# Start-up of a two-layer encoder: input transfers in tile pairs, squares and their sum off POOL, bias table with its rows outermost

## The chip, the core and the metric

The kernel runs on one core of a Trainium2 chip. The metric is the device time of one execution in microseconds (us). A core has five engines with an instruction queue each: PE (TensorE, matrix multiplies, whose weight loads are shown as PEld), DVE (VectorE), ACT (ScalarE), POOL (GpSimd) and SP (SyncE, which issues all DMA transfers here). Sixteen DMA engines carry the transfers.

## The reference

An encoder of two layers over 512 positions of width 1024, all in float32. What matters for this change is the first layer's mixer:

```python
h = x
for l in range(DEPTH):
    hn = rms_norm(h, norm_mix[l])
    if l % 2 == 0:
        ...
        h = h + even_mixer(hn, w_in_even[e], w_out_even[e], lam, ...)
    else:
        h = h + odd_mixer(hn, w_in_odd[o], sg_norm[o], sg_w[o], sg_b[o], w_out_odd[o])
    h = h + swiglu(rms_norm(h, norm_ffn[l]), w_ffn_in[l], w_ffn_out[l])
return rms_norm(h, norm_final)
```

`even_mixer` projects the normed input to eight streams. Four heads go through a gated recurrence in two directions (queries, two gates `zf` and `zb`, values), four through differential attention with a bias by relative position: `bias = rel_bias[rel_bucket(k_pos - q_pos)]`. `rms_norm` needs the mean of the squares over all 1024 features of each position.

## The kernel before, in words

Features lie on the partitions: a tile is 128 features by 512 positions, and the input `xT` is eight such tiles, stored as four pairs. Every product is made of three matmuls of 128x128 by 128x512, since each float32 operand is split into a high part (`fp32r`, cast on ACT) and a low part (a subtraction on DVE): high by high, high by low, low by high. The weights are split on the chip in the same way as they arrive: `weight` (L360) issues a transfer of 512 KB into `raw`, casts it to `whi` and subtracts to `wlo`; for the first weight this is done in two halves, each with a transfer of its own (L367 to L375).

Nothing is issued in the order of the source. `Plan.op` (L80) records each operation with an engine, an estimated cost, the tiles that it reads and writes, and a priority; `Plan.schedule` (L110) then runs a model of the five queues and writes out the order of each engine, the lowest priority number first among what is ready, with limited numbers of tiles of each kind. A DMA counts as its size over 360 KB/us and is taken to land 2 us later. Operations with `port` set are kept apart in the model between DVE and POOL (L189). Without a priority an operation has its place in the source; transfers of weight `i` have -1e6 + 10 i. The first part of the kernel is made of:

- L350: the table `colt` (gains, 25 KB) is loaded ahead of the plan.
- L528 to L533: the input, eight transfers of 256 KB, with priorities among those of the first three weights. Each tile goes to `Norm.add` (L488), which makes the split of x times its gain (`x_m`: ACT, L502, then DVE, L503) and calls `Norm.square` (L507).
- `Norm.square`: for the first two tiles of the first norm the square is a multiply on POOL (L510), else an ACT instruction (L512). The sum over eight tiles is six adds on POOL (L518) and a last one on DVE (L520). The same class serves all four norms ahead of the mixers and feed-forward layers (`m0`, `f0`, `m1`, `f1`). For the first norm the squares and adds have priority 150, so they come after everything of that stage.
- `rstat` (L417): the sum goes over the partitions on PE (`st_m`), then a power on POOL and a product that spreads the result (`sp_m`), which becomes `R_m`, the scale by which all projections are multiplied.
- L535 to L575: masks, lambdas and the one-hot table are loaded, and the bias of each head by relative position is made by two small products `u` into `ut` (4 rows of 1024).
- `store_table` (L577): `ut` goes to DRAM as `ud` (4 x 1024), and one transfer DRAM to DRAM writes it 128 times as `um` (4 heads x 128 rows x 1024, 2 MB). Both sides of that transfer have the 4 heads outermost. The attention heads read skewed rows of `um` far later.
- `gla` (L587) is called for two heads (projections q, zf, zb of 8 steps with 3 matmuls each); then `values` (L720) projects the values `vi` from the four parts of `wev`, 512 KB each; `gla_core` (L598) is a long chain of small steps (`km` on ACT, `lv` on PE, `W` on DVE and POOL, `att` on DVE).

All transfers stand in SP's one queue in the planned order.

Of the kernel before, what the change touches and what calls it, by code (L numbers as in the profile page):

```python
# [13 lines left out]
ALU = mybir.AluOpType  # L14
# [200 lines left out]
def encoder_kernel(  # L215
# [131 lines left out]
    um = dp.tile([4, P, D], F32, name="um")  # L347
    hgn = colt[:, 41:42]

    nc.sync.dma_start(colt, cols)  # L350
    make_identity(nc, ident)
    G.memset(ones, 1.0)
    G.memset(mhalf, -0.5)
# [6 lines left out]
    def weight(src):  # L360
        i = weights[0]
        weights[0] += 1
        n = src.shape[-1]
        raw = buf("raw", f"raw{i}")
        hi = buf("whi", f"whi{i}", F32R)
        lo = buf("wlo", f"wlo{i}", F32R)
        step = n // 2 if i == 0 else n  # L367
        for c in range(0, n, step):
            pr = -1e6 + i * 10 + c * 0.005
            cut = lambda ap, c=c: ap[:, c:c + step]  # L370
            pa = c // step if step < n else None
            dma(raw(cut, pa), src[:, c:c + step], step / 2, prio=pr, after=gate)
            acopy(hi(cut, pa), raw(cut, pa), cost=0.16 + step * 0.00078, prio=pr)
            vtt(lo(cut, pa), raw(cut, pa), hi(lambda ap, c=c: f32(ap)[:, c:c + step], pa), ALU.subtract,
                cost=0.07 + step * 0.00104, prio=pr, either=True)  # L375
        hi.half = lo.half = step < n
        return hi, lo
# [104 lines left out]
    class Norm:  # L482
# [5 lines left out]
        def add(self, h, prio=None):  # L488
            k = self.n
            if self.paired:  # L490
                if k % 2 == 0:
                    self.b = buf("huge", f"b_{self.name}{k}", shape=(P, 8, H))
                s0 = 2 - 2 * (k % 2)
                act(self.b(lambda ap: ap[:, s0:s0 + 2].rearrange("p a c -> p (a c)"), part=1 - k % 2), h, AF.Copy, scale=colt[:, self.gain * KC + k:self.gain * KC + k + 1],
                    cost=0.61, prio=URGENT + len(plan.ops))
                if k % 2:
                    self.xs.append(operands(self.b, f"{self.name}{k}"))
                self.square(h, prio)
                return
            g = colt[:, self.gain * KC + k:self.gain * KC + k + 1]  # L500
            xp = buf("big", f"x_{self.name}{k}", F32R)
            act(row(xp, 0), h, AF.Copy, scale=g, cost=0.61)  # L502
            vstt(row(xp, 1), h, g, frow(xp, 0), ALU.mult, ALU.subtract)  # L503
            self.xs.append(xp)
            self.square(h, prio)

        def square(self, h, prio=None):  # L507
            sq = buf("tmp", f"sq_{self.name}{self.n}")
            if self.gain == 0 and self.n < 2:
                gtt(sq, h, h, ALU.mult, prio=prio)  # L510
            else:
                act(sq, h, AF.Square, prio=prio)  # L512
            self.n += 1
            if self.sq is None:
                self.sq = sq
                return
            if self.n < KC:
                gtt(self.sq, self.sq, sq, ALU.add, prio=prio)  # L518
                return
            vtt(self.sq, self.sq, sq, ALU.add)  # L520
            if self.gain in (0, 2):
# [3 lines left out]
            else:  # L525
                self.R = rnorm(self.sq, D, self.name, "R")

    n0 = Norm(0, "m0")  # L528
    for j in range(KC // 2):
        xt = buf("big", f"xin{j}")  # L530
        for i in range(2):
            dma(row(xt, i), xT[j][:, i], 256, prio=-1e6 + (0.5, 2, 3, 11, 12, 21, 22, 23)[2 * j + i])
            n0.add(row(xt, i), 150)  # L533

    maskf = buf("big", "maskf", shape=(P, 7, P))  # L535
    dma(maskf, masks, 448, prio=-1e6 + 95)
# [22 lines left out]
    lt = buf("tmp", "lt", shape=(P, 256))  # L559
    lprod = buf("tmp", "lprod", shape=(P, 128))  # L560
    dma(lt, lams.partition_broadcast(P), 128, prio=-1e6 + 96)
    op_tiny = plan.op("DVE", 2.0, tiny, [lprod], [lt])

    oht, ut = buf("big", "oht", shape=(P, D)), buf("big", "ut", shape=(P, D))

# [10 lines left out]

    def store_table():  # L577
        nc.sync.dma_start(ud, ut.ap()[0:4])
        nc.sync.dma_start(um, bass.AP(ud.tensor, ud.offset, [[D, 4], [0, P], [1, D]]))

    op_um = plan.op("DMA", 6.0, store_table, [], [ut], prio=200)

# [639 lines left out]
```

## Time and profile before

| | |
|---|---|
| median of 3 runs | 1203.88 us (1202.47 to 1203.91) |
| the profiled execution, its own time | 1204.61 us |
| its span in the trace | 1202.8 us |
| PE busy | 1163.3 us, 97% |
| DVE busy | 915.4 us, 76% |
| ACT busy | 579.1 us, 48% |
| POOL busy | 188.0 us, 16% |
| moved by DMA | 118.58 MB, mean 99 GB/s |
| granted TensorE clock, mean | 0.995 |

The span runs from the first instruction to the last; the time of the execution is 1.8 us longer. An engine is busy while an instruction of it runs; idle time is put down to what ended it. In the views below a line such as "7.04 1.65 PE L329 MATMUL q<-x_m,whi ... x2 [7.04 <-ACT x_m L322]" reads: at 7.04 us, for 1.65 us, on PE, two instructions from line 329 that write `q` and read `x_m` and `whi`; in brackets how long the engine had been idle and what it waited for.

### The profile page before, as it was taken

To read this page: it belongs to the slowest core of one execution; us is meant where nothing else is said; L and a number is where in the kernel's file an instruction comes from. 1 tells how busy PE (TensorE), PEld (TensorE's weight loads), DVE (VectorE), ACT (ScalarE), POOL (GpSimd) and SP (SyncE) were. 2 spreads that over 40 slices of the span, in tenths; PEclk is the share of its full clock that TensorE was granted. 3 is DMA by queue.
4 is the path that set the end of the run, shared out by engine and by line. 5 is a ranking of instruction groups with operands and counts; after the bars stand their busy time and mean duration, and the time that the engine had idled before them with its cause. 6 is when DMAs were issued, how large, how long until landed. Compare 5 with 4: busy or idle time off the path is not lost.

```text
span 1202.8 us, 17650 instructions
## 1 busy us (share of the span) xinstructions
PE 1163.3 (97%) x7072; PEld 1031.0 (86%) x7072; DVE 915.4 (76%) x1304; ACT 579.1 (48%) x881; POOL 188.0 (16%) x185
## 2 busy tenths in 40 slices
PE   6989999999999999999999999999999999999997
PEld 3868888778778999999999888878899999999996
DVE  5467698769697997777777873757799778877874
ACT  5244465657554544444444444335555444444444
POOL 4355584213130000000000040003000000000003
PEclk9989999999999999999999999999999999999998
DMA  6420420343415232424233423330333232323302
GB/s 217 165 82 1 111 81 10 91 123 88 158 35 174 81 106 70 141 71 141 71 140 106 141 78 98 88 105 5 148 110 133 71 132 79 108 102 106 105 1 71
DMA packets 28686, 118.58 MB, mean 99 GB/s; under 512 B 5272, under 2 KB 7448, under 8 KB 20412
## 3 DMA queue, kind: packets, MB, share of 16 engines
q1 hardware_dynamic: 28604, 117.46, 29.5%
q8 instruction: 55, 0.90, 0.3%
q14 instruction: 27, 0.22, 0.1%
HBM read 115.30 MB, written 4.23 MB: 99 GB/s over the span
## 4 chain that ended last, share of the span: by engine, by line
PE 80%; DMA 7%; DVE 6%; issue 4%; ACT 2%; POOL 1%; SPq 0%; POOLq 0%; DVEq 0%; ACTq 0%
PE fo_0b L329 8%; PE fo_0a L329 8%; PE uo L329 4%; PE oo L329 4%; PE vo L329 3%; PE lv L657 2%; DMA raw<-wev 2%; PE fo_18a L329 2%; PE vi L329 2%; PE last L329 1%; PE q L329 1%; PE zf L329 1%; PE zb L329 1%; PE oe L329 1%; DMA xin<-xT 1%
## 5 line engine op out<-in xcount | busy, mean ns | idle before, releaser
L298 DVE TENSOR_TENSOR wlo<-raw,whi 128x1024 fp32r<-128x1024 f32 (+1 forms) x65 | 85.4, 1314 | 29.5 <-ACT whi L317 29.4
L298 DVE TENSOR_TENSOR lb<-comb,hb 128x1024 fp32r<-128x1024 f32 x44 | 53.7, 1220 | 38.5 <-ACT hb L317 38.5
L317 ACT CAST whi<-raw 128x1024 fp32r<-128x1024 f32 (+1 forms) x65 | 66.8, 1031 | 22.3 <-DMA raw<-wev 10.7
L298 DVE TENSOR_TENSOR la<-raw,ha 128x1024 fp32r<-128x1024 f32 x44 | 55.0, 1249 | 27.1 <-ACT ha L317 26.9
L317 ACT CAST hb<-comb 128x1024 fp32r<-128x1024 f32 x44 | 46.1, 1048 | 59.7 <-PE pa9a L948 2.4
L310 POOL TENSOR_TENSOR sq_m<-sq_m,sq_m 128x512 f32<-128x512 f32 x12 | 19.9, 1657 | 328.9 <-ACT sq_m L322 328.4
L317 ACT CAST ha<-raw 128x1024 fp32r<-128x1024 f32 x44 | 46.2, 1049 | 48.8 <-PE pa10a L948 2.4
L298 DVE TENSOR_TENSOR l<-raw,h 128x1024 fp32r<-128x1024 f32 (+1 forms) x48 | 54.5, 1136 | 17.0 <-ACT h L317 15.4
L317 ACT CAST hc<-comb 128x1024 fp32r<-128x1024 f32 x44 | 46.1, 1047 | 37.3 <-PE fo_0b L329 15.5
L298 DVE TENSOR_TENSOR comb<-comb,raw 128x512 f32<-128x512 f32 x88 | 62.4, 709 | 0.1
L317 ACT CAST h<-raw 128x1024 fp32r<-128x1024 f32 (+1 forms) x48 | 46.6, 975 | 27.9 <-PE pb4b L948 2.0
L310 POOL TENSOR_TENSOR sq_fin<-sq_fin,sq_fin 128x256 f32<-128x256 f32 x12 | 8.9, 738 | 327.2 <-ACT sq_fin L322 326.8
L687 POOL TENSOR_TENSOR W<-W,T 128x512 f32<-128x512 f32 x38 | 52.7, 1394 | 39.7 <-PE lv L657 35.5
L298 DVE TENSOR_TENSOR lc<-comb,hc 128x1024 fp32r<-128x1024 f32 x44 | 54.7, 1244 | 2.2 <-ACT hc L317 2.2
L924 DVE TENSOR_TENSOR comb<-raw 128x1024 f32<-128x1024 f32 x44 | 54.7, 1243 | 0.0
L329 PE MATMUL vo<-whi,x_m 128*128 128x512 f32 x128 | 40.3, 391 | 0.1
L329 PE MATMUL uo<-x_m,whi 128*128 128x512 f32 x128 | 40.1, 394 | 0.0
L329 PE MATMUL oo<-mx,whi 128*128 128x512 f32 x128 | 39.6, 390 | 0.0
L657 PEld LDWEIGHTS lv<-W,km 128*128 128x128 f32 x224 | 31.4, 196 | 8.6 <-ACT km L650 6.2
L317 ACT CAST hd<-raw 128x512 fp32r<-128x512 f32 x44 | 27.4, 622 | 22.4 <-PE pa0a L948 2.0
L657 PE MATMUL lv<-W,km 128*128 128x128 f32 x224 | 32.5, 290 | 5.8 <-ACT km L650 5.8
L310 POOL TENSOR_TENSOR sq_f<-sq_f,sq_f 128x512 f32<-128x512 f32 x12 | 20.2, 1686 | 103.1 <-ACT sq_f L322 103.1
(2624 smaller groups left out, 4208.7 us busy)
## 6 DMA issues: line engine op xcount, KB each, us to landing
raw<-wfi SPq DMA_DIRECT2D x44, 1024.0 KB, 4.9
raw<-wfo SPq DMA_DIRECT2D x20, 1024.0 KB, 4.9
raw<-we SPq DMA_DIRECT2D x23, 512.0 KB, 5.2
raw<-wev SPq DMA_DIRECT2D x8, 512.0 KB, 12.4
raw<-woe SPq DMA_DIRECT2D x8, 512.0 KB, 3.8
raw<-wov SPq DMA_DIRECT2D x8, 512.0 KB, 3.7
raw<-wo SPq DMA_DIRECT2D x8, 512.0 KB, 3.6
raw<-woo SPq DMA_DIRECT2D x8, 512.0 KB, 3.7
```

The costliest lines, as they stand in the source:

```text
L298: return plan.op("DVE", cost, lambda: V.tensor_tensor(use(o), use(a), use(b), op), [o], [a, b], prio=prio, after=after, alt=alt, port=insi ...
L310: return plan.op("POOL", cost, lambda: G.tensor_tensor(use(o), use(a), use(b), op), [o], [a, b], prio=prio)
L317: return plan.op("ACT", cost, lambda: A.copy(use(o), use(a)), [o], [a], prio=prio)
L329: T.matmul(use(o), lhsT=use(l), rhs=use(r), start=s0, stop=s1)
L657: T.matmul(blk(ps.ap(), b), lhsT=blk(km.ap(), b), rhs=mixed(0, b * P, P, s)(W.ap()), start=True, stop=True)
L687: return lambda: eng.tensor_tensor(view(W.ap()), view(W.ap()), fn(TT.ap()), ALU.mult)
L924: plan.op("DVE", 1.14, lambda: V.tensor_tensor(comb.ap()[:, 0:2], raw.ap()[:, 0:1].broadcast_to([P, 2, S]), raw.ap()[:, 1:3], ALU.add), [c ...
```

## The change

Four things are edited. The first weight is loaded by one transfer and still split in two halves. `colt` becomes a planned transfer right behind it (`op_cols`), on which the first uses of `colt` depend. The input comes in four transfers of a tile pair, 512 KB each, with priorities 0.5, 6, 11 and 12 (the second and third weight have 10 and 20), and the squares and adds of the first norm get priority 20 in place of 150. All squares are made on ACT and all adds on DVE, in all four norms of this class. The DRAM to DRAM transfer to `um` has the 128 rows outermost on both sides, and the 4 heads inside them; the rows themselves (4 KB each, 512 of them) stay.

```diff
@@ -347,7 +347,6 @@
     um = dp.tile([4, P, D], F32, name="um")
     hgn = colt[:, 41:42]
 
-    nc.sync.dma_start(colt, cols)
     make_identity(nc, ident)
     G.memset(ones, 1.0)
     G.memset(mhalf, -0.5)
@@ -369,7 +368,8 @@
             pr = -1e6 + i * 10 + c * 0.005
             cut = lambda ap, c=c: ap[:, c:c + step]
             pa = c // step if step < n else None
-            dma(raw(cut, pa), src[:, c:c + step], step / 2, prio=pr, after=gate)
+            if c == 0:
+                dma(raw, src, n / 2, prio=pr, after=gate)
             acopy(hi(cut, pa), raw(cut, pa), cost=0.16 + step * 0.00078, prio=pr)
             vtt(lo(cut, pa), raw(cut, pa), hi(lambda ap, c=c: f32(ap)[:, c:c + step], pa), ALU.subtract,
                 cost=0.07 + step * 0.00104, prio=pr, either=True)
@@ -499,23 +499,20 @@
                 return
             g = colt[:, self.gain * KC + k:self.gain * KC + k + 1]
             xp = buf("big", f"x_{self.name}{k}", F32R)
-            act(row(xp, 0), h, AF.Copy, scale=g, cost=0.61)
+            act(row(xp, 0), h, AF.Copy, scale=g, cost=0.61).deps.add(op_cols)
             vstt(row(xp, 1), h, g, frow(xp, 0), ALU.mult, ALU.subtract)
             self.xs.append(xp)
             self.square(h, prio)
 
         def square(self, h, prio=None):
             sq = buf("tmp", f"sq_{self.name}{self.n}")
-            if self.gain == 0 and self.n < 2:
-                gtt(sq, h, h, ALU.mult, prio=prio)
-            else:
-                act(sq, h, AF.Square, prio=prio)
+            act(sq, h, AF.Square, prio=prio)
             self.n += 1
             if self.sq is None:
                 self.sq = sq
                 return
             if self.n < KC:
-                gtt(self.sq, self.sq, sq, ALU.add, prio=prio)
+                vtt(self.sq, self.sq, sq, ALU.add, prio=prio)
                 return
             vtt(self.sq, self.sq, sq, ALU.add)
             if self.gain in (0, 2):
@@ -525,12 +522,13 @@
             else:
                 self.R = rnorm(self.sq, D, self.name, "R")
 
+    op_cols = plan.op("DMA", 0.45, lambda: nc.sync.dma_start(colt, cols), prio=-1e6 + 0.2)
     n0 = Norm(0, "m0")
     for j in range(KC // 2):
         xt = buf("big", f"xin{j}")
+        dma(xt, xT[j], 512, prio=-1e6 + (0.5, 6, 11, 12)[j])
         for i in range(2):
-            dma(row(xt, i), xT[j][:, i], 256, prio=-1e6 + (0.5, 2, 3, 11, 12, 21, 22, 23)[2 * j + i])
-            n0.add(row(xt, i), 150)
+            n0.add(row(xt, i), 20)
 
     maskf = buf("big", "maskf", shape=(P, 7, P))
     dma(maskf, masks, 448, prio=-1e6 + 95)
@@ -559,7 +557,7 @@
     lt = buf("tmp", "lt", shape=(P, 256))
     lprod = buf("tmp", "lprod", shape=(P, 128))
     dma(lt, lams.partition_broadcast(P), 128, prio=-1e6 + 96)
-    op_tiny = plan.op("DVE", 2.0, tiny, [lprod], [lt])
+    op_tiny = plan.op("DVE", 2.0, tiny, [lprod], [lt], after=[op_cols])
 
     oht, ut = buf("big", "oht", shape=(P, D)), buf("big", "ut", shape=(P, D))
 
@@ -576,7 +574,7 @@
 
     def store_table():
         nc.sync.dma_start(ud, ut.ap()[0:4])
-        nc.sync.dma_start(um, bass.AP(ud.tensor, ud.offset, [[D, 4], [0, P], [1, D]]))
+        nc.sync.dma_start(um.rearrange("h p d -> p h d"), bass.AP(ud.tensor, ud.offset, [[0, P], [D, 4], [1, D]]))
 
     op_um = plan.op("DMA", 6.0, store_table, [], [ut], prio=200)
 
```

## Rows read from the trace of the kernel before

**Rows 1.** The page, busy time, share of the span, instructions of each engine.
```profile
PE 1163.3 (97%) x7072; PEld 1031.0 (86%) x7072; DVE 915.4 (76%) x1304; ACT 579.1 (48%) x881; POOL 188.0 (16%) x185
```

**Rows 2.** The chain that ended last, to 70 us: start us, us, what.
```profile
13.90 7.56 DMA rbt<-rel_bias
...
38.26 23.07 DMA raw<-wev
```

**Rows 3.** Stretches: us; busy (count) of PE, PEld, DVE, ACT, POOL; clock, DMA share, GB/s.
```profile
2.00:7.00 5.00, 0.00 (x0) 0.00 (x0) 0.69 (x1) 1.36 (x4) 0.75 (x1) 1.00 0.92 250
7.00:14.00 7.00, 4.04 (x6) 1.58 (x6) 3.37 (x3) 6.56 (x10) 5.75 (x5) 1.00 1.00 380
14.00:21.60 7.60, 6.23 (x12) 3.54 (x13) 7.40 (x5) 3.58 (x7) 6.70 (x5) 1.00 1.01 338
...
25.00:30.00 5.00, 5.00 (x14) 3.91 (x14) 2.39 (x11) 3.03 (x4) 0.00 (x0) 1.00 0.00 0
...
42.00:46.00 4.00, 4.00 (x19) 3.30 (x18) 2.58 (x4) 3.97 (x6) 1.10 (x2) 1.00 0.26 105
...
50.00:54.00 4.00, 4.00 (x21) 3.54 (x20) 1.79 (x2) 0.70 (x1) 3.50 (x3) 1.00 1.02 381
```

**Rows 4.** Instructions in order of time, 0 to 64 us.
```profile
7.04 1.65 PE L329 MATMUL q<-x_m,whi 128*128 128x512 f32 x2 [7.04 <-ACT x_m L322]
...
15.34 8.49 DVE L302 SCALAR_TENSOR_TENSOR x_m<-xin,colt,x_m 128x512 fp32r<-128x512 f32 x7
...
17.17 0.80 PE L329 MATMUL q<-x_m,whi 128*128 128x512 f32 x1 [0.47 <-DVE x_m L302]
...
21.60 3.57 PE L329 MATMUL u<-oht,rbt 32*4 32x512 f32 x4 [0.65 <-DMA rbt<-rel_bias]
...
28.68 0.63 PE L329 MATMUL zb<-x_m,wlo 128*128 128x512 f32 x1
...
29.68 0.39 PE L329 MATMUL q<-x_m,wlo 128*128 128x512 f32 x1
...
37.41 0.74 SPq L579 DMA_DIRECT2D um<-ud  x1
```

**Rows 5.** The second transfer of `wev`, issued at 38.26 us: time from issue to landing.
```profile
DMA to landing us min/median/max: 23.1/23.1/23.1
```

**Rows 6.** Instructions in order of time, 41 to 71 us.
```profile
61.41 1.04 ACT L317 CAST whi<-raw 128x1024 fp32r<-128x1024 f32 x1 [10.70 <-DMA raw<-wev]
...
66.79 2.08 PE L657 MATMUL lv<-W,km 128*128 128x128 f32 x8 [5.77 <-ACT km L650]
...
70.59 0.62 PE L329 MATMUL vi<-whi,x_m 128*128 128x512 f32 x2
```

**Rows 7.** The chain that ended last, behind the stall: start us, us, what.
```profile
74.40 0.89 PE lv L657 x8
...
78.00 3.46 PE vi L329 x15
```

**Rows 8.** POOL and DVE in the second norm (`f0`), in order of time.
```profile
330.59 3.93 POOL L310 TENSOR_TENSOR sq_f<-sq_f,sq_f 128x512 f32<-128x512 f32 x2 [13.92 <-ACT sq_f L322]
...
331.04 2.32 DVE L298 TENSOR_TENSOR la<-raw,ha 128x1024 fp32r<-128x1024 f32 x1
...
333.28 0.68 DVE L298 TENSOR_TENSOR h<-h,oe 128x512 f32<-128x512 f32 x1
...
359.86 1.21 DVE L298 TENSOR_TENSOR la<-raw,ha 128x1024 fp32r<-128x1024 f32 x1
```

**Rows 9.** Longer stretches behind the start (columns as in rows 3).
```profile
80.00:100.00 20.00, 20.00 (x121) 17.66 (x120) 13.91 (x18) 8.32 (x13) 12.65 (x13) 1.00 0.09 28
...
260.00:280.00 20.00, 18.93 (x86) 14.29 (x86) 18.45 (x41) 16.20 (x31) 2.59 (x3) 1.00 0.56 164
...
340.00:360.00 20.00, 18.39 (x95) 15.19 (x93) 20.00 (x27) 11.50 (x17) 4.23 (x3) 1.00 0.15 52
```

**Rows 10.** DVE's waits, 70 to 345 us: us in total, times, longest.
```profile
DVE on L302 <- DMA R_b<-dr_b: 10.6, 3, 6.7
```

## Prediction

> **What bounds the kernel now.** I read the page first: PE is busy 97% of the span [rows 1], so about 40 us of it are PE idle, and what PE loses beyond that is time at its lower clock level. Both lie mostly in the first 70 us. From 80 to 160 PE is busy all the time (the row of 80 to 100 is the first of four that say so [rows 9]), in the order that the planner wrote, so what is won before carries through to the end as long as nothing else becomes late.
>
> The chain of waits shows where those 70 us go [rows 2]: the small table `rbt`, which lands at 21.46 (13.90 + 7.56), PE work, and then 23.07 us in which the second part of `wev` is on its way.
>
> The stretches and the order of time show the first loss [rows 3, 4]. The first matmul starts at 7.04. PE then does 6 matmuls to 14 us and 12 to 21.6, four of `u`, and 14 to 30. The clock column reads 1.00 there, but a matmul of 512 columns takes 0.63 us up to 28.68 and 0.39 from 29.68 on, at a pace of 0.43 and 0.23 (15 in 3.46 us [rows 7]): PE is at the lower level, 1.2 GHz, until 29.3. The 32 matmuls by 30.0 are worth 32 x 0.23 = 7.4 us at the upper level, the four of `u` half of 3.57, so 9.2 us of work took 30.0 - 7.04 = 23.0: **13.8 us lost**. The transfers are at full share from 2 to 21.6 [rows 3], and DVE needs 8.49 us, to 23.8, for seven low parts of x, 1.21 each [rows 4], in a stretch in which POOL is busy for 6.70 of 7.60 us, mostly with the adds of squares [rows 3].
>
> The second loss is the stall. `um` is issued at 37.41 [rows 4]. Behind it the DMA share is 0.26 at 105 GB/s, where two other stretches have 1.0 at 380 [rows 3]: about 4 of 16 engines work. The transfer of `wev` issued right behind it lands after 23.1 us [rows 5]. ACT's cast waits 10.70 us for it [rows 6], DVE's queue stands behind the cast, and with it the `W` step, `km` and `lv`. Between 61.0 (66.79 less the wait of 5.77) and 70.59 [rows 6] PE does eight `lv` and five `vi` matmuls. At the upper level they take 0.89 + 5 x 0.23 = 2.05 [rows 7]; they took 9.6: **7.6 us lost**, 5.8 idle and the rest at the lower level behind it.
>
> **The change part by part.** The bias table. The same 2.1 MB in the same 512 rows of 4 KB go out with 128 outermost. At 105 GB/s they take 20 us; at the 381 of the stretch 50 to 54, whose rows of weights are also 4 KB, 5.5. Its two ends are these: no gain, or all of it. I take the second, as the share of 0.26 fits an outermost count of 4 and nothing else in the row. Then `um` ends near 45 at the latest, and the `wev` part, 0.5 MB, lands by 48, against a use near 61; even if PE gets there 8 us sooner, 5 us of cover are left. The stall goes, -7.6. Late next is the chain `W`, `km`, `lv`, which no longer stands behind the cast; PE's `vi` matmuls lie between its steps. No row has a DRAM to DRAM transfer over all engines, hence the end at zero. The Trainium skill, page "DMA: Bandwidth & Descriptors", section "Rules for kernel authors", says that an outermost dimension of c below 16 keeps a transfer on at most c engines and wants a multiple of 16 there; the row of 0.26 agrees, and by the rule 128 gets all sixteen.
>
> The transfers. Five issues of about 0.43 us fall away on SP, one fewer for the first weight and four for the input; they are worth nothing, since from 2 us on the engines are loaded. `colt` behind the first weight starts that weight some 0.4 us sooner. But the first matmul now needs the whole first weight and the whole first pair, 1.07 MB instead of 0.55. At the 250 GB/s of the first stretch that is 4.3 us from 2.0, and with 1 us to land and a cast of 0.65 the first matmul starts at 7.9; at the 380 of the second stretch, at 6.5. Against 7.04 that is -0.5 to +0.9; I take +0.3. The pairs bring two steps of work at once, so PE starts with six matmuls, not three. The last input lands about 1.4 us sooner, because the third weight, 0.5 MB at 380 GB/s, now stands behind it. The bytes ahead of `rbt` stay the same, so it still lands near 21.
>
> Squares and sum. ACT gets two squares, DVE six adds in the first stage, and POOL is empty. The low parts of x then need not wait for POOL: the nearest row is a DVE instruction of 128x512 at 0.68 [rows 8], in place of 1.21. By the priorities as written (20 against the place in the source, which is 23, 28 and 32 for the high parts of the sixth to eighth tile) ACT makes all squares ahead of these three casts; that puts the last low part near 19 to 20 us, 3 to 4 sooner than before. Working the order through by hand, PE has some 14 steps of three matmuls ahead of `u` in its queue, where it had 6 (18 matmuls by 21.6 [rows 3]). A step takes 1.28 us at the lower level and 0.69 at the upper. Before, six steps and `u` were done at 25.17, and three more steps ran at the lower level, at a loss of 3 x 0.59 = 1.8. Case one, the upper level from about 13 us on: PE reaches `u` when `rbt` lands, near 21.5, and `u` is done in half its time, at 23.3; 1.9 sooner, eight steps ahead (8 x 0.69 = 5.5) and without the 1.8, it is **9** us ahead. Case two, the lower level all the way: 7.3 + 14 x 1.28 = 25.2, `u` done at 28.8; 3.6 later, with 5.5 and 1.8 won, **4** ahead. Ends of this part: +0.9 (nothing but the later first matmul) and -9; I take **-6** with the first matmul's +0.3 in it.
>
> Which of the two depends on the clock. Before, PE was at work from 17.17 on with one gap of 0.65 us ahead of `u`, and stayed at the lower level until 29.3 [rows 4]; behind the stall, at 70.59, it was back at the upper level 3.8 us after its restart [rows 6]. So the rows allow both, -4 and -9. The Trainium skill, page "TensorE: Matmul & The Clock Gate", section "Part 1", has it that the clock rises once PE has been busy for a sustained while and falls back after idling; by this rule alone the level rises well ahead of `u`, and the sum would be some 3 us lower, while the first case here ran longer at the lower level than that lets one expect.
>
> The three later norms. In `f0` DVE is busy all of 340 to 360 while PE has 1.6 us idle [rows 9], and six POOL adds fall into DVE's work. The subtraction beside two of them takes 2.32 us, alone 1.21 [rows 8]: 1.1 longer. On DVE an instruction of 128x512 takes 0.68 [rows 8]. Six are 4.1 more against up to 6.6 less, net -2.5; the other end is +4.1, should the stretched rows have another cause. PE's idle time there is small, so of the 2.5 I count **-1.5**. In `m1` PE has no gap and in `f1` little, so nothing is counted; cover gone, each add is 0.68 on a DVE busy for 76% [rows 1]. The final norm keeps POOL. The new order of the plan elsewhere: 0, between +2 and -2.
>
> **Sum:** -7.6 - 6 - 1.5 = -15.1. The profiled execution took 1204.6 (span 1202.8), so 1189.5; the median of the runs is 0.7 lower, so **1189**.
>
> **Rivals.** (a) *The start does not gain.* The casts of three tiles stand behind all squares, the second and third weight come later, and PE waits where it computed before. For: the first stretch moves only 250 GB/s, and PE's queue is in order. Against: six of the first 24 steps done by 25 us is little to lose. Left: -7.6 - 1.5 + 0.9, 1196.
>
> (b) *The table does not do what it says*: the 512 descriptors still go over few engines, or reading four rows from everywhere is slow. For: no row shows such a transfer at speed. Then the stall stays and 1.5 + 6 are won: 1196 to 1197.
>
> (c) *The gain is given back in the attention stage.* From 260 to 280 DVE is busy 18.45 of 20 and PE idles [rows 9]. If DVE sets the pace from 160 to 360, PE only arrives sooner to wait. For: these rows. Against: from 60 to 160 DVE has a quarter of its time free, so it comes forward too. Half of 13.6 lost: 1196; all of it: 1202.
>
> (d) *Slower.* The planner counts a landing at 2 us, but DVE waits up to 6.7 us for `R_b`, read back from DRAM, and its queue stands still meanwhile [rows 10]. In a new order more work may stand behind such a wait, PE runs dry and restarts at the lower level. One costs up to 6.7; three more are 20, and the time is 1204 - 15 + 20 = 1209. It decides from 2.3 of them. Against: three now cost 10.6 together, and PE hardly idles behind them.
>
> **How the numbers follow.** The forecast has 0.64, (a) 0.15, (b) 0.08, (c) 0.07, (d) 0.06. The forecast's own range is -9 - 7.6 - 2.5 - 2 = -21.1 to -4 - 7.6 + 1 = -10.6, that is 1182.8 to 1193 (the lower end is rounded down to 1182); with (a) and (b) the upper end goes to 1198, where the rest of (c) and (d) is left out. A difference of 0.2%, 2.4 us, is about what can be told from no change here. Faster by more: the forecast, (a), (b) and most of (c), 0.91; within: 0.03; slower: 0.06.
>
> **What would show it.** Right: a DMA share near 1 for some 5 us behind `um`, `wev` landing within 10 us, no PE gap near 60, a matmul of 0.39 us before 25 us, low parts of x at 0.7 each, DVE steps of `f0` without 2.3 us ones. Wrong: a share of 0.25 for 20 us behind `um`; PE gaps between 10 and 20 us as long as now; or PE reaching the `vi` products 10 us sooner and the residual stage near 320 no sooner.

## The result, and the profile after

The changed kernel takes 1184.24 us (median of four runs, 1181.48 to 1186.74); the kernel before took 1203.40 in its four. The ratio is 0.9842, with a 95% interval of 0.9829 to 0.9856: 19.2 us less. The forecast was 1189, with a range of 1182 to 1198. The profiled execution of after took 1181.48 (span 1179.7 against 1202.8), so its trace shows 23.1 us gained; it is the fastest of the four, and a part of the spread has a cause that comes out below.

The page's busy rows of after answer to [rows 1]: PE's busy time fell by 10.7 us (the same 7072 matmuls, more of them at the upper clock level), its idle time by 12, and POOL has 28 instructions fewer.

```profile
PE 1152.6 (98%) x7072; PEld 1030.1 (87%) x7072; DVE 914.1 (77%) x1330; ACT 578.0 (49%) x881; POOL 148.7 (13%) x157
```

The stretches of after, with the columns of [rows 3]: the first three and 25 to 30 stand against the same rows of before, the two of 35 to 45 against the one of 42 to 46, since `um` is now issued 5 us sooner.

```profile
2.00:7.00 5.00, 0.00 (x0) 0.00 (x0) 1.29 (x2) 1.62 (x4) 0.00 (x0) 1.00 0.87 316
7.00:14.00 7.00, 6.69 (x16) 4.98 (x17) 6.15 (x9) 7.00 (x13) 0.00 (x0) 1.00 1.03 417
14.00:21.60 7.60, 7.60 (x30) 4.78 (x29) 7.19 (x12) 3.81 (x7) 1.19 (x1) 1.00 0.97 324
25.00:30.00 5.00, 5.00 (x26) 4.24 (x27) 3.38 (x6) 0.43 (x1) 3.60 (x1) 1.00 0.02 3
35.00:40.00 5.00, 4.99 (x22) 3.83 (x21) 3.62 (x5) 4.97 (x9) 1.95 (x2) 1.00 0.99 311
40.00:45.00 5.00, 5.00 (x23) 4.14 (x23) 3.53 (x4) 2.99 (x5) 5.00 (x5) 1.00 0.97 365
...
200.00:205.00 5.00, 1.67 (x9) 1.33 (x8) 4.91 (x8) 4.11 (x7) 1.04 (x1) 0.94 0.42 168
205.00:210.00 5.00, 3.64 (x12) 2.43 (x11) 3.60 (x7) 3.83 (x7) 0.00 (x0) 0.72 0.00 0
```

PE does 16 and 30 matmuls where it did 6 and 12, and 26 where it did 14. Behind `um` the DMA share is 0.97 to 0.99 in place of 0.26. The last two rows are of the attention stage: near 200 us PE stands still for most of 5 us, and the clock column falls to 0.94 and 0.72, which is (0.06 + 0.28) x 5 / 0.5 = 3.4 us at the lower level.

The timeline of the start, in order of time, answers to [rows 4].

```profile
7.31 1.58 PE L329 MATMUL q<-x_m,whi 128*128 128x512 f32 x2 [7.31 <-ACT x_m L322]
...
11.59 2.18 ACT L322 ACTIVATE sq_m<-xin 128x512 f32<-128x512 f32 x4
...
12.53 0.63 PE L329 MATMUL q<-x_m,wlo 128*128 128x512 f32 x1
...
13.28 0.42 SPq L566 DMA_DIRECT2D rbt<-rel_bias  x1
...
13.57 0.39 PE L329 MATMUL zf<-x_m,wlo 128*128 128x512 f32 x1
...
13.75 0.42 SPq L287 DMA_DIRECT2D raw<-we  x1
...
15.67 1.93 ACT L322 ACTIVATE x_m<-xin,colt 128x512 fp32r<-128x512 f32 x3
...
18.86 1.40 DVE L302 SCALAR_TENSOR_TENSOR x_m<-xin,colt,x_m 128x512 fp32r<-128x512 f32 x2
...
19.35 1.88 PE L329 MATMUL u<-oht,rbt 32*4 32x512 f32 x4
...
32.14 0.67 SPq L577 DMA_DIRECT2D um<-ud  x1
```

A matmul of 512 columns takes 0.39 from 13.57 on, where before it did from 29.68 on; PE has no gap over 0.4 us from 7.31 to 200. Seven of the eight low parts of x take 0.75 or less (the line has 1.40 for the last two); the 1.21 of the kernel before mixes four of 1.45 to 1.77 and three of 0.74. All squares come ahead of the last three casts of x on ACT. `rbt` is issued ahead of the sixth weight (13.28 against 13.75), where before all six weights stood ahead of it, and `u` starts at 19.35. The DMA view of 10 to 45 us gives the median time from issue to landing as the last number of a line:

```profile
raw<-wev SPq DMA_DIRECT2D x4, 512.0 KB, 8.6
um<-ud SPq DMA_DIRECT2D x1, 2048.0 KB, 9.4
...
rbt<-rel_bias SPq DMA_DIRECT2D x1, 0.5 KB, 5.6
```

So `rbt` lands at 18.9 (21.5 before), and `um` takes 9.4 us. The stall of [rows 6] is gone.

The timeline near 200 us shows what was given back.

```profile
194.19 0.33 SPq L287 DMA_DIRECT2D R_b<-dr_b  x1
...
199.41 0.75 DVE L302 SCALAR_TENSOR_TENSOR on<-or_b,colt,R_b 128x512 f32<-128x512 f32 x1 [3.49 <-DMA R_b<-dr_b]
...
202.88 0.69 DVE L685 TENSOR_TENSOR W<-W,T 128x512 f32<-128x512 f32 x1
...
203.72 3.08 PE L329 MATMUL pf<-W 128*128 128x256 f32 x8 [3.33 <-DVE W L685]
...
208.59 0.50 PE L798 MATMUL s<-Kl,QK 128*128 128x512 f32 x1 [1.36 <-DVE Kl L771]
```

DVE waits 3.49 us for `R_b`, read back from DRAM; the `W` step stands behind it in DVE's queue, and PE's `pf` waits 3.33 us for `W`. The wait of DVE is not new. In the kernel before the same step of the same head waited longer, but what stood behind it held PE for 2.07 us only, and the clock stayed up:

```profile
220.55 0.75 DVE L302 SCALAR_TENSOR_TENSOR on<-or_b,colt,R_b 128x512 f32<-128x512 f32 x1 [6.73 <-DMA R_b<-dr_b]
...
221.96 0.50 PE L329 MATMUL o_b<-al,vih 128*128 128x512 f32 x1 [2.07 <-DVE al L298]
```

What is new is that the order puts `W` and `pf` behind it.

Where along the kernel the time went is seen from when PE starts its k-th matmul, in us, worked out from the traces (PE does the same 7072 in each; every column is one execution, and e7 is the changed kernel once more):

```
k       before   after      e1      e2      e3      e4      e5      e7      e9     e10     e11     e12
0         7.04    7.31    8.25    5.99    8.83    6.66    8.25    8.02    8.00    6.76    5.82    8.32
100      44.08   33.32   34.07   42.04   38.08   36.53   33.72   33.75   33.05   37.74   34.52   33.85
150      54.94   45.03   45.78   52.90   49.80   46.81   45.42   45.46   44.75   49.47   45.39   45.58
200      72.19   54.48   65.10   62.52   59.26   56.11   54.88   54.92   54.21   58.93   59.52   55.03
700     167.39  149.40  160.07  157.72  154.22  154.35  149.85  149.89  149.17  153.89  154.70  150.00
1000    228.40  212.14  223.79  215.53  218.94  212.09  214.59  214.64  209.71  216.92  214.32  212.11
1300    295.66  277.48  288.74  282.62  284.09  284.25  279.87  280.33  274.73  282.40  281.75  277.27
1500    341.25  321.02  332.25  328.16  327.60  331.11  323.37  323.84  318.26  325.91  327.35  320.78
2000    416.58  393.98  405.51  404.24  404.55  403.88  400.52  396.84  391.33  399.25  401.35  393.76
7000   1184.69 1161.72 1173.21 1172.10 1172.32 1173.03 1168.48 1164.97 1159.96 1167.08 1169.40 1161.46
```

After is ahead by 10.8 us at matmul 100, 17.7 at 200 and 18.0 at 700; at 1000 it is 16.3, for the wait at 200 us lies between. From 1300 to 2000, the first output projection and the first feed-forward norm, the lead grows from 18.2 to 22.6, and stays at 23. In e7 the lead is 17.3 at 200, 13.8 at 1000, 15.3 at 1300 and 19.7 from 2000 to the end, near the 19.2 of the medians.

### The profile page after: what moved, and what is told of

Its sections match the earlier page's. It is cut to its first block, busy times and chain, and to the rows that moved or that the text cites. A ratio compares the mean times of both kernels' runs of the same rounds, so it can differ in the third digit from the quotient of the medians.

```text
span 1179.7 us, 17607 instructions
## 1 busy us (share of the span) xinstructions
PE 1152.6 (98%) x7072; PEld 1030.1 (87%) x7072; DVE 914.1 (77%) x1330; ACT 578.0 (49%) x881; POOL 148.7 (13%) x157
## 4 chain that ended last, share of the span: by engine, by line
PE 72%; DVE 4%; ACT 1%; issue 1%; POOLq 0%; POOL 0%; DVEq 0%; ACTq 0%
PE fo_0b L329 8%; PE fo_0a L329 8%; PE uo L329 4%; PE oo L329 4%; PE vo L329 4%; PE fo_18a L329 2%; PE last L329 1%; PE oe L329 1%; PE g L329 1%; DVE h L298 1%; PE mix L329 1%; DVE wlo L298 1%; DVE xlv_f L476 1%; PE o_a L329 0%; PE pa1b L946 0%
## 5 line engine op out<-in xcount | busy, mean ns | idle before, releaser
L298 DVE TENSOR_TENSOR wlo<-raw,whi 128x1024 fp32r<-128x1024 f32 (+1 forms) x65 | 82.1, 1267 | 13.1 <-ACT whi L317 12.3
L298 DVE TENSOR_TENSOR la<-raw,ha 128x1024 fp32r<-128x1024 f32 x44 | 53.9, 1225 | 28.4 <-ACT ha L317 28.2
L317 ACT CAST whi<-raw 128x1024 fp32r<-128x1024 f32 (+1 forms) x65 | 66.7, 1033 | 13.3 <-PE vo L329 6.4
L298 DVE TENSOR_TENSOR l<-raw,h 128x1024 fp32r<-128x1024 f32 (+1 forms) x48 | 54.5, 1135 | 16.9 <-ACT h L317 15.3
L685 POOL TENSOR_TENSOR W<-W,T 128x512 f32<-128x512 f32 x36 | 47.4, 1325 | 47.4 <-PE lv L655 42.3
L310 POOL TENSOR_TENSOR rr_m<-ms_m,mhalf 128x4 f32<-128x4 f32 x2 | 4.6, 2301 | 349.3 <-DVE ms_m L306 349.3
L659 DVE COPY_PREDICATED att<-maskt,lv 128x512 f32<-128x512 uint8 x28 | 20.8, 742 | 16.6 <-PE lv L655 14.2
L685 DVE TENSOR_TENSOR W<-W,T 128x512 f32<-128x512 f32 x28 | 31.2, 1119 | 3.0 <-PE pa L329 1.4
L648 ACT COPY km<-W 128x512 f32<-128x512 f32 x28 | 18.6, 663 | 29.3 <-POOL W L685 9.1
```

The source lines that it names most:

```text
L298: return plan.op("DVE", cost, lambda: V.tensor_tensor(use(o), use(a), use(b), op), [o], [a, b], prio=prio, after=after, alt=alt, port=insi ...
L310: return plan.op("POOL", cost, lambda: G.tensor_tensor(use(o), use(a), use(b), op), [o], [a, b], prio=prio)
L317: return plan.op("ACT", cost, lambda: A.copy(use(o), use(a)), [o], [a], prio=prio)
L648: plan.op("ACT", 0.52, lambda km=km, s=s: A.copy(km.ap().rearrange("p (n two s) -> p n two s", two=2, s=s), mixed(1, 0, S, s)(W.ap())), [k ...
L659: plan.op("DVE", 0.6, lambda ps=ps, li=li: V.copy_predicated(att.ap().rearrange("p (b c) -> p b c", b=NB), maskt[:, li:li + 1].broadcast_t ...
L685: return lambda: eng.tensor_tensor(view(W.ap()), view(W.ap()), fn(TT.ap()), ALU.mult)
```

## The experiments

Every kernel here computes the whole reference. Diffs are against the changed kernel unless said otherwise; the ratio is to the kernel before on the same chip, with its 95% interval.

**The table undone.**

```diff
-        nc.sync.dma_start(um.rearrange("h p d -> p h d"), bass.AP(ud.tensor, ud.offset, [[0, P], [D, 4], [1, D]]))
+        nc.sync.dma_start(um, bass.AP(ud.tensor, ud.offset, [[D, 4], [0, P], [1, D]]))
```

> The changed kernel with the old order of dimensions in the transfer to um (heads outermost), nothing else. Theory: the table alone was worth the stall, so it comes back: a DMA share of 0.26 for some 20 us from 32 us on, the two last parts of wev landing near 56 us instead of 44, ACT's casts behind them (planned for 44 us) late by 10 us, PE idle for 4 to 8 us, and the time is 1188 to 1192. Rival: with the new start two of the four parts of wev are already there before um is issued and the values' matmuls that need the others start only after 58 us, so the time stays within 2 us of the changed kernel, 1182 to 1187.

1196.35 us, ratio 0.9943 (0.9924 to 0.9961): 12 us slower than the changed kernel, more than either expectation. The stall is back, and longer than before: ACT's cast waits 12.04 us for `wev`, PE 7.39, and the stretch of 55 to 60 has a DMA share of 0.26 again (columns of the stretches as above).

```profile
57.17 1.04 ACT L317 CAST whi<-raw 128x1024 fp32r<-128x1024 f32 x1 [12.04 <-DMA raw<-wev]
...
60.13 0.79 PE L329 MATMUL vi<-whi,x_m 128*128 128x512 f32 x1 [7.39 <-DVE zz L298]
```
```profile
55.00:60.00 5.00, 0.00 (x0) 0.00 (x0) 1.76 (x3) 1.53 (x2) 0.00 (x0) 0.50 0.26 106
...
60.00:65.00 5.00, 4.87 (x14) 4.01 (x15) 2.58 (x5) 3.81 (x6) 2.54 (x4) 0.50 0.44 159
```

Here `um` goes out 4.5 us sooner than in the kernel before and PE comes 9.2 sooner (matmul 150), so it stands longer behind the slow transfer. The start is as in the changed kernel (matmul 100 at 34.07), so it doesn't hang on the table.

**The table alone**, the same edit the other way, in the kernel before.

> The kernel before with the new order of dimensions in the transfer to um, nothing else. Theory: the gap of 5.8 us near 61 us and the low clock level behind it go, 7.6 us, so 1196 (1194 to 1198), with the start as before. Rival: the recurrence's chain is late next and takes half of it, 1199 to 1201; or, if reading the four rows from all engines is slow, 1203.

1192.41, ratio 0.9914 (0.9892 to 0.9936), 9.6 us less and below the range that was expected. From matmul 150 to 200 it takes 9.62 us, before 17.25: 7.6, the term of the sum to the tenth. The start hardly moves: matmul 100 at 42.04, 2.0 sooner, half of it a first matmul that came 1 us sooner. Between 700 and 1000 the lead grows by another 3.2; PE's gap of 2.07 at 219.9 in the kernel before is gone there, and DVE's wait for `R_b` at this place is 3.56 us in place of 6.73. That sum, 12.8, is this one execution's; the medians differ by 9.6.

**POOL's work back**, all four norms.

```diff
-            act(sq, h, AF.Square, prio=prio)
+            if self.gain == 0 and self.n < 2:
+                gtt(sq, h, h, ALU.mult, prio=prio)
+            else:
+                act(sq, h, AF.Square, prio=prio)
...
-                vtt(self.sq, self.sq, sq, ALU.add, prio=prio)
+                gtt(self.sq, self.sq, sq, ALU.add, prio=prio)
```

> The changed kernel with squares and adds as before on POOL, in all four norms; transfers, priorities and table as changed. Theory: taking POOL's adds away gave about 6 us in the second norm and its output projection, and some 3 us at the start, where DVE's low parts of x stretch to 1.2 us again: 1191 to 1195. Rival: the gain at the start and in the second norm came from the other order of the plan and not from POOL: within 2 us of the changed kernel, 1182 to 1187.

1191.19, ratio 0.9898 (0.9873 to 0.9923): 7 us slower, inside the expectation. Two PE gaps are back in the start, and behind them the clock falls from 20.6 to 24.0:

```profile
15.04 0.50 PE L329 MATMUL zf<-x_m,wlo 128*128 128x512 f32 x1 [0.59 <-DVE wlo L298]
...
18.44 1.87 PE L329 MATMUL u<-oht,rbt 32*4 32x512 f32 x4 [0.81 <-DMA rbt<-rel_bias]
```

Matmul 100 is 4.8 us later, 1.5 of it from the first matmul; matmuls 1500 to 2000 take 76.95 us in place of 72.96. In this execution the wait for `R_b` also holds PE for 5.25 us, as in the longer execution of the changed kernel. But the start does not go back to where it was: with all of POOL's work in place the upper level is there from 13.8 to 20.6, and matmul 100 is still 6.0 us ahead of the kernel before.

**POOL's work taken away alone**, the reverse of that diff in the kernel before.

> The kernel before with squares on ACT and adds on DVE in all four norms, nothing else (the priorities, the transfers and the table as before). Theory: POOL's part alone is worth its 3 to 4 us in the second norm, and 2 to 4 at the start, while the stall behind um stays: 1194 to 1198. Rival: without the other transfers and with the stall the start's gain is used up waiting for wev: 3 to 4 us only, 1198 to 1200.

1189.99, ratio 0.9891 (0.9872 to 0.9909): 13.6 us, more than expected. Matmul 100 starts at 34.52, 9.6 sooner than before: this part alone brings nearly all of the start's gain (and the run with POOL's work back has 6.0 without it, so the parts overlap). The upper level is there from 11.6 us on, and 45 matmuls stand ahead of `u` (18 before, 39 after). The stall is shorter too, since `um` is issued at 29.92:

```profile
53.83 1.04 ACT L317 CAST whi<-raw 128x1024 fp32r<-128x1024 f32 x1 [3.83 <-DMA raw<-wev]
...
55.53 1.78 PE L654 MATMUL lv<-W,km 128*128 128x128 f32 x8 [2.70 <-ACT km L647]
```

Two things change with this edit: DVE's low parts no longer share time with POOL, and the planner, whose model keeps DVE and POOL apart, orders steps sooner. The runs do not divide the gain between them. From matmul 1300 to 2000, where the later norm is, this kernel takes 119.60 us, the one before 120.92 and the changed one 116.50: of the 4.4 us won there 1.3 come with this part alone.

**Adds of the three later norms back on POOL.**

```diff
-                vtt(self.sq, self.sq, sq, ALU.add, prio=prio)
+                (gtt if self.gain else vtt)(self.sq, self.sq, sq, ALU.add, prio=prio)
```

> The changed kernel with the adds of the later norms (f0, m1, f1) back on POOL; the first norm's stay on DVE. Theory, from the run with all of POOL's part put back (4 us of its 8 behind the output projection and the second norm): 4 us slower than the changed kernel, 1186 to 1189, with DVE instructions of 2.3 us in the second norm again and the start as in the changed kernel. Rival: the loss of that run in the second norm came from its late start and another order of the plan: no difference, 1182 to 1185.

1187.52, ratio 0.9874 (0.9857 to 0.9891), against 1184.43 for the changed kernel on the same chip: 3.1 us. Beside a POOL add a DVE step of 128x1024 takes 2.31 again; in the changed kernel such a step takes 1.22, and the add 0.68 on DVE:

```profile
321.35 1.47 POOL L310 TENSOR_TENSOR sq_f<-sq_f,sq_f 128x512 f32<-128x512 f32 x1 [3.44 <-ACT sq_f L322]
...
321.59 2.31 DVE L922 TENSOR_TENSOR comb<-raw 128x1024 f32<-128x1024 f32 x1
```

And in the changed kernel, same norm:

```profile
322.48 0.68 DVE L298 TENSOR_TENSOR h<-h,oe 128x512 f32<-128x512 f32 x1
323.07 1.22 DVE L298 TENSOR_TENSOR lb<-comb,hb 128x1024 fp32r<-128x1024 f32 x1
...
324.55 0.68 DVE L298 TENSOR_TENSOR sq_f<-sq_f,sq_f 128x512 f32<-128x512 f32 x1
```

**The input in eight transfers and the first weight in two**, at the old priorities.

```diff
-            if c == 0:
-                dma(raw, src, n / 2, prio=pr, after=gate)
+            dma(raw(cut, pa), src[:, c:c + step], step / 2, prio=pr, after=gate)
...
-        dma(xt, xT[j], 512, prio=-1e6 + (0.5, 6, 11, 12)[j])
         for i in range(2):
+            dma(row(xt, i), xT[j][:, i], 256, prio=-1e6 + (0.5, 2, 3, 11, 12, 21, 22, 23)[2 * j + i])
```

> The changed kernel with the input in eight transfers and the first weight in two, at the old priorities; squares and adds off POOL and the table as changed. Theory: the order of the transfers made PE's queue start with six matmuls and no gaps, which brought the clock up at 13 us instead of 29; without it PE has its gaps between 9 and 17 us again and the clock rises after 20 us: 4 to 8 us slower than the changed kernel, 1188 to 1192. Rival: the gaps came from POOL beside DVE, and the transfers are worth nothing: 1182 to 1187.

1190.58, ratio 0.9903 (0.9881 to 0.9926). The number fits, the mechanism does not: the start is only 3.2 us later at matmul 100, with one gap of 0.46, and the clock rises at 15.3, not after 20 (it falls again from 25.5 to 29.0). The rest comes with another order of the plan far behind it: from matmul 1000 to 1500 it loses 10.1 us. Two of its PE gaps:

```profile
86.95 1.16 PE L654 MATMUL lv<-W,km 128*128 128x128 f32 x8 [1.44 <-ACT km L647]
...
219.32 0.44 PE L816 MATMUL pt<-ident,pr 128*128 128x128 f32 x2 [2.58 <-DVE mn L801]
```

**The same order with small transfers**: the first weight and each pair go out in two transfers of 256 KB, issued in one planned step at the same place.

```diff
-            if c == 0:
+            if c == 0 and step < n:
+                def halves():
+                    for b in (0, step):
+                        nc.sync.dma_start(raw.ap()[:, b:b + step], src[:, b:b + step])
+                plan.op("DMA", n / 720, halves, [raw], [], after=gate, prio=pr)
+            elif c == 0:
...
-        dma(xt, xT[j], 512, prio=-1e6 + (0.5, 6, 11, 12)[j])
+        def rows_(xt=xt, j=j):
+            for i in range(2):
+                nc.sync.dma_start(xt.ap()[:, i], xT[j][:, i])
+        plan.op("DMA", 512 / 360, rows_, [xt], [], prio=-1e6 + (0.5, 6, 11, 12)[j])
```

> The changed kernel with each input pair and the first weight issued as two transfers of 256 KB in place of one of 512 KB, at the same places of the plan; the order on the other engines is unchanged. Theory: what counted in the transfers was the order that the plan made of them, not their number or size: the time is within 1.5 us of the changed kernel, 1183 to 1186, and PE's first matmul within 0.7 us of its. Rival: fewer transfers with rows of 4 KB are what helps: five more issues of 0.43 us and rows of 2 KB delay the start by 2 us or more, 1186 to 1189.

1183.61, ratio 0.9836 (0.9815 to 0.9856): the changed kernel's time, with four executions from 1181.16 to 1186.79. In these medians the number and size of the transfers are worth nothing that can be told. The profiled execution is the slowest of the four, and its start shows what the rival expected: the added issues put `rbt` 1.1 us later (14.39 against 13.28), PE waits for it, and the clock is down from 21.7 to 28.6.

```profile
14.39 0.42 SPq L574 DMA_DIRECT2D rbt<-rel_bias  x1
```
```profile
20.61 2.48 PE L329 MATMUL u<-oht,rbt 32*4 32x512 f32 x4 [1.05 <-DMA rbt<-rel_bias]
```

Its matmul 100 starts at 37.74, 4.4 us later than in the changed kernel. Whether the three faster executions had this wait is not shown.

**The priority of squares and adds back at 150.**

```diff
-            n0.add(row(xt, i), 20)
+            n0.add(row(xt, i), 150)
```

> The changed kernel with priority 150 in place of 20 for the squares and adds of the first norm. Theory: the priority is worth little: ACT's casts of the sixth to eighth tile come 3 us sooner, R_m some us later, PE is full from 13 us on either way: within 2 us of the changed kernel, 1181 to 1186. Rival: the early R_m is what let the recurrence start at 37 us instead of 43, and without it the chain waits: 3 to 6 us slower, 1186 to 1190.

1184.98, ratio 0.985 (0.983 to 0.9869): no difference. The wait at 200 us is gone in this order, and a gap of 1.40 at 34.9 and one of 1.56 at 299.2, in the output projection, have come in its place; behind neither does the clock fall.

**The changed kernel once more**, unedited, to see the spread.

> The changed kernel itself, once more, on the chip of the other runs. Its four runs before lay at 1181.5 and 1186.7 with mean clocks of 0.996 and 0.992. Theory: the wait of 3.3 us at 200 us lets the clock fall for one stretch of 3.4 us or for longer, by chance: the times lie between 1181 and 1187, and the profile has a low stretch there whose length goes with the time (10 us of it where the time is 5 us longer). Rival: the difference comes from the transfers at the start, and the low stretch is 3.4 us in any run.

1184.43, ratio 0.9852 (0.9834 to 0.987). This profiled execution took 1184.73, with the same three lines near 200 us and a longer wait:

```profile
201.06 1.61 DVE L302 SCALAR_TENSOR_TENSOR on<-or_b,colt,R_b 128x512 f32<-128x512 f32 x1 [4.63 <-DMA R_b<-dr_b]
...
205.34 0.69 DVE L685 TENSOR_TENSOR W<-W,T 128x512 f32<-128x512 f32 x1
...
206.18 3.75 PE L329 MATMUL pf<-W 128*128 128x256 f32 x8 [5.24 <-DVE W L685]
```
```profile
205.00:210.00 5.00, 3.83 (x9) 2.87 (x9) 3.58 (x6) 4.94 (x9) 0.00 (x0) 0.50 0.02 3
```

PE waits 5.24 in place of 3.33, and the stretch behind it is at the lower level throughout. From matmul 900 to 1000 it takes 28.4 us, 26.4 in the first profile, so this wait makes 2 of the 3.25 us between the two executions.

**The planner told what a round trip takes** (4 to 5.5 us for the transfers of the heads' norms in place of 2).

```diff
...
-                lat = 2.0 if e == "DMA" else LATENCY
+                lat = (o.lat or 2.0) if e == "DMA" else LATENCY
...
-        dma(c, line(lambda ap: ap[0:1]), 20)
+        dma(c, line(lambda ap: ap[0:1]), 20).lat = 4.0
...
+        o.lat = 4.0
...
-        dma(R, dr.broadcast_to([P, S]), 256, after=[o])
+        dma(R, dr.broadcast_to([P, S]), 256, after=[o]).lat = 5.5
```

> The changed kernel with the planner told how long the norms' round trip through DRAM takes (4 us for the two small transfers and 5.5 us for the rows spread from DRAM, instead of 2 us each); the work is the same, only the planned order differs. Theory: DVE's queue stands behind R_b less (3.5 us at 199 us in the changed kernel), PE's wait of 3.3 us near 200 us and the low clock level behind it go: 1177 to 1181. Rival: the waits move to other places of the attention stage, where DVE is near full, and the time is 1181 to 1187.

1193.44, ratio 0.9918 (0.9897 to 0.994): 9 us slower than the changed kernel on the same chip, and the theory fell. The new order starts the output projection 14 us sooner (270.1 against 283.8) and then stretches it from 49 us to 70. A truer latency alone does not make this planner's order better.

**DVE's `on` step behind `W`**: the one instruction that waits for `R_b` is put five DVE instructions later by hand.

```diff
+        order = plan.schedule()
+        late = gla_end[2]
+        i = order.index(late)
+        order.pop(i)
+        n = 0
+        while n < 5:
+            n += order[i].eng == "DVE"
+            i += 1
+        order.insert(i, late)
-        for o in plan.schedule():
+        for o in order:
```

> The changed kernel with one instruction of the plan moved by hand: on DVE, the product of the third recurrence head that waits for R_b (issued at 195.9 us, started at 199.4 in the changed kernel) goes five DVE instructions later, behind the W update that PE's pf waits for. Every other engine's order is kept. Theory: the new wait of the changed kernel is DVE's queue standing behind R_b; with the move PE's gap of 3.3 to 5.2 us near 200 us shrinks below 1.5 us, the clock doesn't fall there, and the time is 4 to 7 us below the changed kernel, 1177 to 1180. Rival: W was late for another reason (its own chain through lv), PE's gap stays within 1 us of what it was, and the time is 1183 to 1186.

1181.86 (1179.71 to 1182.37), ratio 0.982 (0.9806 to 0.9834). Its interval overlaps that of the changed kernel; the medians differ by 2.4 to 2.6 us, about half of what was expected, and the clock still falls there (202.5 to 205.9). The trace shows why:

```profile
200.36 1.54 DVE L685 TENSOR_TENSOR W<-W,T 128x512 f32<-128x512 f32 x1
201.82 0.74 DVE L302 SCALAR_TENSOR_TENSOR on<-or_b,colt,R_b 128x512 f32<-128x512 f32 x1
...
202.04 3.29 PE L329 MATMUL pf<-W 128*128 128x256 f32 x8 [1.88 <-DVE W L685]
```

`W` no longer waits for the transfer, but PE still waits 1.88 us for `W` itself, which needs the `pa` product just ahead of it. This kernel has the lowest median here.

**That gap too**: in the kernel of the last experiment `pa` goes two value steps earlier and `W` ahead of the DVE steps of `QK`, by hand in the same list.

```diff
...
+        dve = [o for o in order[i + 1:] if o.eng == "DVE"][:5]
+        order.remove(late)
+        order.insert(order.index(dve[3]) + 1, late)
+        order.remove(dve[4])
+        order.insert(order.index(dve[2]), dve[4])
+        pa = next(o for o in order if o.eng == "PE" and any(b.name == "pa_3" for b in o.bufs))
+        pe = [o for o in order if o.eng == "PE"]
+        order.remove(pa)
+        order.insert(order.index(pe[pe.index(pa) - 2]), pa)
...
```

> As e9_on_behind_w, and two more instructions of the planned order moved by hand: PE's pa products of the fourth recurrence head go two values steps (six matmuls, 1.4 us) ahead, and DVE's W update that waits for them stands ahead of the two QK subtractions; the product that waits for R_b stands behind these. Theory: what was left of PE's wait near 200 us (1.9 us in e9) was the chain pa, W, pf with nothing of PE's work between pa and pf; with six matmuls between them the wait is below 0.5 us, the clock doesn't fall there any more, and the time is 3 to 4 us below e9, 1177 to 1180. Rival: the W update ahead of QK makes the scores late instead: PE waits 1.5 us or more for Kl behind pf, the clock falls as before, and the time is that of e9, 1180 to 1183.

1182.00, ratio 0.9828 (0.9813 to 0.9844): the same as without it; the rival was right. `pf` now waits 0.38, and `s` stands 2.64 behind the next product of DVE:

```profile
201.40 1.99 PE L329 MATMUL pf<-W 128*128 128x256 f32 x8 [0.38 <-POOL W L685]
...
206.96 0.50 PE L798 MATMUL s<-Kl,QK 128*128 128x512 f32 x1 [2.64 <-DVE Kl L771]
```

In these rows DVE's chain sets the pace, and moving a step only moved the gap; the clock is down from 207.8 to 211.2.

## Why the prediction was right, step by step

The direction and the mechanism of the table and of the start were right, and the median lies inside the forecast's own range, 4.8 us under its number and 2.2 above its lower end. Two terms were too small, and one loss was not counted. The sizes of the start, of `f0` and of the order are read from the fastest execution, whose trace gained 23.1 us and whose own time, 1181.48, lies just below the range; in the second one, e7, the start has 10.3 and `f0` the same 4.4, and the wait at 200 us costs 2 us more.

*The table, -7.6.* Measured alone 7.6 (matmuls 150 to 200). The share of 0.97 to 0.99 in place of 0.26, with nothing but the order of the dimensions edited, shows that this order was what held it. That it is the outermost count agrees with the rule of the Trainium skill (page "DMA: Bandwidth & Descriptors", section "Rules for kernel authors"). Too good was the 5.5 us: `um` took 9.4 from issue to landing, 9.1 alone, and the `wev` parts behind it 10.8. The cover held it all the same.

*The start, -6, between -4 and -9.* Measured -10.8. Case one came true, and by hand most of it fits: 39 matmuls, 13 steps, ahead of `u` (14 predicted), the squares ahead of three casts of x, the last low part done at 20.3 (19 to 20), the upper level at 13.3 (13). What failed is the sentence "The bytes ahead of `rbt` stay the same, so it still lands near 21": SP now issues `rbt` ahead of the sixth weight, it lands at 18.9, and `u` ends at 21.2 and not at 23.3. The choice of a value between the cases was too cautious as well. How the 10.8 divide between the parts is not settled: with POOL's work taken away alone 9.6 of it came, and with everything but that 6.0, so either brings most of it and the two overlap. No run has the transfers or the priorities alone; with the transfers in halves at the same places the median was the same, and the one start that was profiled 4.4 us later.

*The first matmul, +0.3, between -0.5 and +0.9.* 7.31 against 7.04 in the two first profiles, but a single execution does not tell: the nine with whole pairs started between 7.19 and 8.83 (mean 8.0), the four with eight transfers at the old priorities between 5.82 and 7.04 (mean 6.4). The pairs in halves at the changed places started at 6.76. So the pairs, with the first weight in one transfer, cost some 1.6 us here, more than the upper end. The 1 us to land in this term stands in none of the rows shown.

*`f0`, -1.5, of -2.5 on DVE.* Mis-sized: the lead grows by 4.4 us from matmul 1300 to 2000, and the adds of the later norms alone are worth 3.1 us of the median. PE's 1.6 us of idle time in one stretch, 340 to 360, was taken as all that could be won; from matmul 1300 to 2000 PE is idle for 5.7 us in the kernel before and for 2.5 in the changed one, and neither falls to the lower level there. Not all of that is POOL's: with its work taken away alone 1.3 us came, near the term, and PE's gaps of 1.2 us in the output projection stayed, which are gone in the changed order. Put back into that order the adds cost more, 4.2 us there: PE is idle for 4.1 us and at the lower level from 340.7 to 347.6.

*Order of the plan, 0 between -2 and +2.* Here lies the wait at 200 us, 1.7 us of lead between matmul 700 and 1000; 1.9 come back by 1300, so in sum little is left of it (in e7 3.7 go and 1.6 come back). It is rival (d)'s mechanism, DVE's queue standing behind the round trip of `R_b`, once and with 3.3 to 5.2 us of PE idle, where three more of 6.7 were needed for its time. Against it the prediction said that PE hardly idles behind these waits; behind the longest, 6.73, it idled 2.07 already. Rival (c) is not what happened: from 260 to 280 PE is busy 19.5 of 20, so DVE does not take back what the start won.

*The parts don't add.* Table alone 9.6 and POOL alone 13.6 are 23.2, against 19.2 for everything: both shorten the same stall, and from matmul 700 to 1000 the table alone won 3.2 us and POOL alone 1.4, where the changed kernel lost 1.7.

## What to carry to other kernels

Read the share of the DMA engines behind a large transfer before anything else; a share of 0.26 told that few engines carried it, and the transfers queued behind it paid. In the first microseconds count PE's gaps together with the clock: in the kernel before five gaps, with DVE's steps stretched beside POOL's, went with 22 us at the lower level, and of the two edits that were run alone, taking POOL's part away won more (13.6 us against 9.6). Where a planner writes the order, a small edit at the start is also a new order 200 us later; look for an in-order queue that stands behind a round trip through DRAM, and for what stands behind it there. One profile is one execution: here a start could be 4.4 us later in the profile and the median the same.

## What the hardware showed that was not expected

The first matmul of nearly the same kernel started anywhere from 5.82 to 8.83 us, and the nine kernels with the same input transfers spread over 1.6 us.

A gap of PE could cost more than its length, but not every gap did. Behind 3.33 us near 200 us the clock was at the lower level for 3.4 us, at 5.24 for 6.8 (203.6 to 210.5, of which 2.5 lie in the gap itself), behind 1.88 for 3.4 (202.5 to 205.9), and at the start of the run with POOL's work back, behind gaps of 0.59 and 0.81, for 3.4 (20.6 to 24.0). Behind 2.07 us in the kernel before (219.9 to 222.0), and behind 1.40 and 1.56 in the run with the squares last, it did not fall at all. So the length of a gap alone does not tell, and no run here shows what does. At the start the level rose 6.0 us after the first matmul in the changed kernel, where PE had no gap over 0.4 us (7.31 to 13.3), 4.5 us after it in its second execution (8.02 to 12.5), and 22 us after it in the kernel before, with its five gaps of 0.47 to 1.89 ahead of `u` and at it. The Trainium skill, page "TensorE: Matmul & The Clock Gate", section "Part 1", says that the clock rises after sustained work and falls back after idling; the rises at the start and the fall at 5.24 us agree, while the falls behind 0.59 and 0.81 stand beside a gap of 2.07 without one. Which of the five gaps kept it down in the kernel before no run here tells.

The second half of the round trip of `R_b`, from the issue of the transfer out of DRAM to the DVE step that waits for it, took 5.2 us in one execution of the changed kernel (194.19 to 199.41) and 6.5 in the other (194.51 to 201.06), in the same instruction order; in the kernel before it took 6.4 (214.14 to 220.55).
